# A hybrid conv/SSD trunk on one core: first z tiles from the raw x, the second block's norm from a token copy, and a hand-written order for the opening stage

## The chip, the cores and the metric

The kernel runs on one core of a Trainium2 chip. The metric is the device time in microseconds, the median of three runs. The core has TensorE (PE, matmuls; PEld is its weight load), VectorE (DVE), ScalarE (ACT), GpSimd (POOL) and SyncE (SP), which issues the DMAs. Each engine takes its instructions in the order of its own queue; semaphores tie the engines together.

## The reference

One layer and a final norm over x of 2048 tokens by 1024 channels, all in float32:

```python
def hybrid_layer(x, norm_mix_w, w_in, ...):
    h = rmsnorm(x, norm_mix_w)                 # x * rsqrt(mean(x*x) + eps) * w, per token
    proj = jnp.einsum("btd,dc->btc", h, w_in)
    u_b, u_c, u_h, z, xbc, dt_raw = jnp.split(proj, SPLITS, axis=-1)
    y_a = short_conv_mixer(u_b, u_c, u_h, short_conv_w)
    y_b = ssd_mixer(z, xbc, dt_raw, ...)       # uses silu(z) as a gate, softplus(dt_raw + dt_bias)
    x = x + jnp.einsum("btc,cd->btd", jnp.concatenate([y_a, y_b], -1), w_out)
    h = rmsnorm(x, norm_mlp_w)
    hid = jnp.square(jax.nn.relu(jnp.einsum("btd,df->btf", h, w_up)))
    return x + jnp.einsum("btf,fd->btd", hid, w_down)
```

The norm multiplies each token by one number r and each channel by a weight. So `h @ w_in` for a token is r times `(x * w) @ w_in`: the multiplication by r can be done before the projection, on its input, or after it, on its output.

## The kernel before

**Layout.** Activations lie with channels on the 128 partitions and tokens along the free axis. Tokens come in four blocks of 512, two blocks to a half. x is loaded in pieces of 128 partitions by two channel groups by 512 tokens (512 KB, 4 KB to a partition); a block has four such pieces, eight channel groups k.

**Precision.** A float32 product is made of three matmuls in a rounded format: every operand is split into a high part (a cast on ScalarE: `uh` for activations, `whi` for weights) and a low part (operand minus high part, on VectorE: `ul`, `wlo`). `mm3` (L113 to L116) issues high by high, high by low and low by high.

**Seven products.** Most of the input projection goes by pairs of column tiles in a seven-product scheme (`chain`): the two blocks of a half and the two halves of the channels form a 2x2 matrix, and four sums and differences of the operands (t1 to t4, made by `begin_sums`) stand beside the blocks b11, b21, b22. A pair has seven products named b11, t1, t2, b21, t3, b22, t4, in this order, each of 4 x 3 matmuls of 128x512 into the accumulators px, py and pw. `combine` makes the weights' sums s12 and s34 from two raw tiles on VectorE and splits them. Which pair follows which is listed in `PAIRS`; `z`, `x`, `b` and `ch` are the kinds of columns.

**The opening stage** (`Proj.start`). Four tiles of the z columns (w_in tiles 24 to 27) are computed without the seven-product scheme, as plain products of 24 matmuls for each block, so that TensorE has work before the sums exist. For each block, `begin_block` squares the four x pieces (ScalarE), adds the squares into `facc` (VectorE, eight at a time one after the other), sums over the partitions with tiny matmuls (`Rstd.reduce`, pst), takes root and reciprocal on 4 columns (`Rstd.root`), spreads the result over the partitions by two matmuls with diagonal matrices (`Rstd.spread`, prb), and copies it to SBUF. Then each channel group is scaled by weight and norm (L480), cast (L206) and split (L207). `group` runs tiles 24, 25, 26 interleaved by channel group, then tile 27, applies SiLU (L522) and stores the gates to DRAM. `dt_part` computes the 16 dt columns (pd, L604) and their softplus and cumulative sums as a chain of some 25 small operations; both blocks' chains run in the opening stage and the first pair. `begin_sums` makes the operands t1 to t4 from the scaled blocks.

**The first half** (`first_half`). The 20 pairs run with `prepare` beside them, a generator that prepares the second half: it loads x again in its channel layout, squares, adds seven times per block on VectorE (L355, L358), splits the sum (`parts`), sums and spreads it at once by two matmuls (`whole`), takes the root and a reciprocal of 128x512 (L173), then builds and stores the operands of the second half. One step of it runs after each of the seven products of a pair.

**What sets the order.** The code is recorded, and a scheduler of the framework places each engine's instructions by priority and readiness; the order in which the generators are advanced decides the priority. It may move a later operation ahead of an earlier one that would wait.

Of the kernel before, what the change touches and what calls it, by code (L numbers as in the profile page):

```python
# [11 lines left out]
F32 = mybir.dt.float32  # L12
F32R = mybir.dt.float32r
AF = mybir.ActivationFunctionType
# [25 lines left out]
def trunk(ctx: ExitStack, tc: tile.TileContext, x, w_in, w_dt, w_out, w_up, w_down, cvec, hrow, out):  # L40
# [45 lines left out]
    def col(base, i):  # L86
        return cv[:, base + i : base + i + 1]
# [21 lines left out]
    def take(it, n=None):  # L109

        return list(itertools.islice((w for w in it if w is not None), n))
# [11 lines left out]
    class Rstd:  # L123
# [17 lines left out]

        def root(self):
            n = self.n
            r = self.pool.tile([P, n], F32, tag="rs", name="rs", bufs=2)
# [47 lines left out]
    class Seven:  # L192
# [139 lines left out]
        def prepare(self, h, src, base, accs=None, held=None):  # L332
# [7 lines left out]
            for bb in range(NBB):  # L340
                if not accs:
# [64 lines left out]
    class Proj(Seven):  # L406
# [4 lines left out]
        PAIRS = "ch0 ch1 b0 x0 x8 ch2 ch3 b2 x2 ch4 ch5 b4 x4 x10 ch6 ch7 b6 x6 z4 z6".split()  # L411
# [26 lines left out]
        def bias(self):  # L438
            nc.sync.dma_start(self.hb, hrow.partition_broadcast(P))
            nc.scalar.activation(self.a_neg, self.a_neg, AF.Exp)  # L440
            nc.vector.tensor_scalar(out=self.a_neg, in0=self.a_neg, scalar1=-1.0, scalar2=None, op0=ALU.mult)
# [11 lines left out]
        def begin_block(self, bb):  # L453

            xt = self.xt[bb]
            st = Rstd(self.up, self.tmp, D, TB)
            acc = self.facc()
            for m, t in enumerate(xt):
                if bb == 0:
                    sq = self.wide("sq")  # L460
                    nc.scalar.activation(sq, t, AF.Square)
                    sq = [sq[:, 0], sq[:, 1]]
                else:
                    sq = [acc if m + i == 0 else self.tmp("sq") for i in range(2)]
                    for i in range(2):
                        nc.scalar.activation(sq[i], t[:, i], AF.Square)
                if m == 0:
                    nc.vector.tensor_tensor(out=acc, in0=sq[0], in1=sq[1], op=ALU.add)
                else:
                    for i in range(2):  # L470
                        nc.vector.tensor_tensor(out=acc, in0=acc, in1=sq[i], op=ALU.add)
                yield
            st.reduce(acc)
            st.root()
            yield
            r = st.spread(acc)
            yield
            for k in range(KD):
                t = xt[k // 2][:, k % 2]
                nc.vector.scalar_tensor_tensor(  # L480
                    out=t, in0=t, scalar=col(C_NMIX, k), in1=r, op0=ALU.mult, op1=ALU.mult
                )
                self.fill(("b11", "b21", "b12", "b22")[2 * bb + k // 4], k % 4, t)
                yield
# [28 lines left out]
        def group(self, bb, ws, tiles, work, tag="mm"):  # L513

            pm = [psum(tag, "pm", accs[tag]) for _ in tiles]
            for k in range(KD):
                for p, i in zip(pm, tiles):
                    mm3(p, ws[i][0][:, k, :], ws[i][1][:, k, :], *self.block(bb, k), k, KD)
                next(work, None)
            for p, i in zip(pm, tiles):  # L520
                o = self.tmp("z")
                nc.scalar.activation(o, p, AF.Silu)  # L522
                nc.sync.dma_start(sz_d[0][:, i, bb * TB : (bb + 1) * TB], o)

        def start(self):

            self.xt = [[self.raw("x0") for _ in range(KD // 2)], []]
            for k, t in zip(range(0, KD, 2), self.xt[0]):
                nc.sync.dma_start(t, x[0, :, k : k + 2])
            ahead = self.plain(w_in, (24, 25, 26))  # L530
            next(ahead)
            work = self.begin_block(0)
            for m in range(KD // 2):
                next(work)
            for m in range(KD // 2):
                t = self.wide("x1")
                nc.sync.dma_start(t, x[1, :, 2 * m : 2 * m + 2])
                self.xt[1].append(t)
            next(work)
            ws = []  # L540
            for _ in range(3):
                ws += take(ahead, 1)
                next(work)
            self.dt_weights()
            for _ in work:
                pass
            work = self.begin_block(1)
            last = self.plain(w_in, (27,))
            next(last)
            for bb in range(NBB):  # L550
                dts = self.dt_part(bb)
                self.group(bb, ws, (0, 1, 2), work)
                if bb == 0:
                    ws += take(last)
                    self.group(bb, ws, (3,), work, "mw")
                    self.bias()
                    for _ in dts:
                        next(work, None)
                    for _ in work:
                        pass  # L560
                    work = self.begin_sums()
                else:
                    ahead = self.weights(0, self.PAIRS[0])
                    next(ahead)
                    next(dts)
                    got = take(ahead, 3)
                    self.group(bb, ws, (3,), work, "mw")
                    got += take(ahead)
                    for _ in dts:
                        next(work, None)  # L570
                    for _ in work:
                        pass
            return got

        def dt_weights(self):
            self.dt_tiles = [self.up.tile([P, TH], F32, tag="cc", name="dts", bufs=2) for _ in range(NBB)]
            raw = self.tmp("rdt")[:, 0 : KD * 16].rearrange("p (k h) -> p k h", k=KD)
            nc.sync.dma_start(raw, w_dt)
            if self.h == 0:
# [15 lines left out]
        def dt_part(self, b):  # L595

            t = self.dt_tiles[b % NBB]
            v, e, d, p = (t[:, 64 * i : 64 * i + 64] for i in range(4))
            ct = t[:, 256:384]
            rows = t[0:64, 384:640].rearrange("p (a l) -> p a l", a=2)  # L600
# [8 lines left out]
            yield  # L609
            pt = psum("tp", "pt", 2)  # L610
# [879 lines left out]
    with ExitStack() as c1:  # L1490
# [40 lines left out]
        late = mlp.prepare(0, x1_d, C_NMLP, proj_out.accs, proj_out.raw)  # L1531
# [36 lines left out]
def _lay_out(inputs):  # L1568
# [27 lines left out]
        x=f("x")[0].reshape(NB, TB, KD, P).transpose(0, 3, 2, 1),  # L1596
        w_in=cols(w_in[:, :5632]),
# [25 lines left out]
```

## Time and profile before

| | us |
|---|---|
| median of three runs | 2651.9 |
| lowest, highest | 2649.34, 2655.21 |
| the profiled execution's own time | 2657.87 |
| its span in the trace | 2656.2 |
| busy TensorE / VectorE / ScalarE | 2602.7 / 1911.3 / 1430.8 |

Times inside the trace count from the start of the span. A timeline row gives start, duration, engine, line, operation, output and inputs, shape and a count of merged instructions; in brackets stands how long the engine idled just before and what released it. A row of the groups by shape ends with busy time, mean nanoseconds of one, and idle time before with its releaser. A row of the windows gives busy time and number of instructions of PE, PEld, DVE, ACT and POOL, then TensorE's granted clock, the share of the DMA engines, and GB/s. Matmuls overlap in the pipeline, so their spacing, not their duration, is the rate.

### The profile page before, as it was taken

The numbers are of one execution on the slowest core, as the hardware profiler recorded it, in microseconds if no ns is written. First come the engines' busy times: TensorE is split into PE (matmuls) and PEld (weight loads), VectorE is DVE, ScalarE is ACT, GpSimd is POOL, SyncE is SP. The second block draws the span as 40 slices with busy tenths as digits, with TensorE's granted clock in tenths as the row PEclk, the third lists the DMA queues.
The fourth block names the chain that finished last, engine by engine and source line by source line (L and its number), as shares of the span: only waits on it lengthen the run. The fifth ranks groups of instructions, "written<-read, shape, count | busy, mean of one in ns | idle before, by whom it ended". The sixth has DMA issues, their size and how long they took to land.

```text
span 2656.2 us, 33508 instructions
## 1 busy us (share of the span) xinstructions
PE 2602.7 (98%) x12026; PEld 2124.7 (80%) x12026; DVE 1911.3 (72%) x2586; ACT 1430.8 (54%) x2176; POOL 147.1 (6%) x162
## 2 busy tenths in 40 slices
PE   7999999999999999999999999999999999999998
PEld 5778888778877877787888888788887888888887
DVE  7997677667667666757777775755557877888985
ACT  6644345766567566767326555655555444444443
POOL 0010000011111001111000000000000000000001
PEclk9999999999999999999999999999999999999999
DMA  3585445655555578877665674654448554665762
GB/s 145 188 307 187 140 143 185 190 170 167 170 159 174 162 246 246 278 219 227 198 225 204 226 268 159 225 176 146 158 151 285 159 157 148 210 214 172 244 206 73
DMA packets 284806, 511.78 MB, mean 193 GB/s; under 512 B 25312, under 2 KB 141024, under 8 KB 284640
## 3 DMA queue, kind: packets, MB, share of 16 engines
q1 hardware_dynamic: 284640, 509.65, 57.7%
q8 instruction: 94, 1.54, 0.2%
q14 instruction: 72, 0.59, 0.1%
HBM read 344.41 MB, written 165.15 MB: 192 GB/s over the span
## 4 chain that ended last, share of the span: by engine, by line
PE 57%; issue 26%; DMA 6%; DVE 4%; ACT 4%; POOL 1%; SPq 1%; POOLq 0%; DVEq 0%; ACTq 0%
PE px L271 9%; PE px L273 9%; PE px L272 9%; PE py L271 4%; PE py L273 4%; PE py L272 4%; PE pm L114 3%; PE pm L115 3%; PE pm L116 3%; PE pw L271 2%; PE pw L272 2%; PE pw L273 2%; DMA dec<-rd_d 1%; DMA ry<-ys_d 1%; ACT whi L101 1%
## 5 line engine op out<-in xcount | busy, mean ns | idle before, releaser
L271 PE MATMUL px<-uh,whi 128*128 128x512 f32 x1672 | 658.2, 394 | 9.1 <-ACT pw L279 5.9
L273 PE MATMUL px<-uh,wlo 128*128 128x512 f32 x1672 | 652.7, 391 | 2.1 <-DVE wlo L102 2.1
L272 PE MATMUL px<-ul,whi 128*128 128x512 f32 x1672 | 652.7, 390 | 0.0
L102 DVE TENSOR_TENSOR wlo<-wraw,whi 128x1024 fp32r<-128x1024 f32 x230 | 234.0, 1017 | 228.2 <-ACT whi L101 223.0
L271 PEld LDWEIGHTS px<-uh,whi 128*128 128x128 f32 x1672 | 314.8, 188 | 84.4 <-ACT pw L279 8.0
L273 PEld LDWEIGHTS px<-uh,wlo 128*128 128x128 f32 x1672 | 314.8, 188 | 69.4 <-DVE wlo L102 2.9
L272 PEld LDWEIGHTS px<-ul,whi 128*128 128x128 f32 x1672 | 314.9, 188 | 63.9
L101 ACT CAST whi<-wraw 128x1024 fp32r<-128x1024 f32 x230 | 203.5, 885 | 282.0 <-PE px L272 194.0
L101 ACT CAST whi<-s 128x1024 fp32r<-128x1024 f32 x210 | 219.4, 1045 | 213.3 <-PE py L272 69.3
L271 PE MATMUL py<-uh,whi 128*128 128x512 f32 x836 | 327.0, 391 | 1.8 <-DVE acc L987 1.4
L272 PE MATMUL py<-ul,whi 128*128 128x512 f32 x836 | 325.6, 389 | 0.0
L273 PE MATMUL py<-uh,wlo 128*128 128x512 f32 x836 | 325.4, 389 | 0.0
L102 DVE TENSOR_TENSOR wlo<-s,whi 128x1024 fp32r<-128x1024 f32 x210 | 255.3, 1216 | 85.2 <-ACT whi L101 82.7
L114 PE MATMUL pm<-uh,whi 128*128 128x512 f32 (+1 forms) x648 | 253.2, 392 | 2.1 <-ACT uh L206 2.1
L115 PE MATMUL pm<-ul,whi 128*128 128x512 f32 (+1 forms) x648 | 249.7, 385 | 0.0
L116 PE MATMUL pm<-uh,wlo 128*128 128x512 f32 (+1 forms) x648 | 248.7, 384 | 0.0
L271 PEld LDWEIGHTS py<-uh,whi 128*128 128x128 f32 x836 | 156.9, 188 | 35.8 <-DVE acc L987 1.8
L273 PEld LDWEIGHTS py<-uh,wlo 128*128 128x128 f32 x836 | 156.8, 188 | 33.2 <-DVE wlo L102 0.4
L272 PEld LDWEIGHTS py<-ul,whi 128*128 128x128 f32 x836 | 157.0, 188 | 32.2
L271 PE MATMUL pw<-uh,whi 128*128 128x512 f32 x418 | 163.7, 392 | 0.7 <-ACT pw L279 0.7
L272 PE MATMUL pw<-ul,whi 128*128 128x512 f32 x418 | 162.9, 390 | 0.0
L273 PE MATMUL pw<-uh,wlo 128*128 128x512 f32 x418 | 162.7, 389 | 0.0
(223 smaller groups left out, 3738.6 us busy)
## 6 DMA issues: line engine op xcount, KB each, us to landing
hid_d<-e SPq DMA_DIRECT2D x96, 512.0 KB, 3.5
rh<-hid_d SPq DMA_DIRECT2D x96, 512.0 KB, 4.4
wraw<-w_in SPq DMA_DIRECT2D x68, 512.0 KB, 3.9
wraw<-w_up SPq DMA_DIRECT2D x64, 512.0 KB, 4.4
wraw<-w_down SPq DMA_DIRECT2D x104, 256.0 KB, 3.6
dec<-rd_d SPq DMA_DIRECT2D x32, 512.0 KB, 5.5
wraw<-w_out SPq DMA_DIRECT2D x32, 512.0 KB, 5.3
x_d<-xt SPq DMA_DIRECT2D x64, 256.0 KB, 3.6
```

The costliest lines, as they stand in the source:

```text
L101: nc.scalar.copy(hi, raw)
L102: eng.tensor_tensor(out=lo, in0=raw, in1=hi.bitcast(F32), op=ALU.subtract)
L114: nc.tensor.matmul(out, whi, hi, start=(k == 0), stop=False)
L115: nc.tensor.matmul(out, whi, lo, start=False, stop=False)
L116: nc.tensor.matmul(out, wlo, hi, start=False, stop=(k == nk - 1))
L271: nc.tensor.matmul(p, hi, h[0], start=bool(first and k == 0), stop=False, **kw)
L272: nc.tensor.matmul(p, hi, h[1], start=False, stop=False, **kw)
L273: nc.tensor.matmul(p, lo, h[0], start=False, stop=(k == len(g) - 1), **kw)
```

## The change

Five things, all in the opening stage but the last two.

1. The first block's four z tiles are computed from x times the weight alone (`unscaled`), without the norm. The products are multiplied by r afterwards, in PSUM or on the way to the gate (`gate`). The first block is then scaled, cast and split a second time (`scaled`) for the pairs.
2. The second block's norm is computed from a second copy of x that the host lays out with tokens on the partitions (`xt`, 128 tokens by 1024 channels). A squaring on ScalarE with a sum along the free axis (`by_token`) gives the sums without additions on VectorE and without a reduction by matmuls.
3. The opening stage's instructions are recorded under `manual_schedule`, so every engine executes them in the order in which `first_columns` writes them. The dt chains (`dt_part`) start at the end of the stage, second block first, and their remaining steps run one after each product of the first pairs.
4. In the first half, `prepare` gets the second half's norms from token copies too, with `root` and `spread` in the place of `parts` and `whole`. It starts with the second pair and advances after three of the seven products.
5. `PAIRS` begins with z4 and x0 in the place of ch0 and ch1.

```diff
     class Rstd:
...
+        def begin_tokens(self):
+            self.sums = self.pool.tile([P, self.n], F32, tag="rs", name="ssum", bufs=3)
+
+        def by_token(self, c, t):
+            nc.scalar.activation(t, t, AF.Square, accum_out=self.sums[:, c : c + 1])
...
         def prepare(self, h, src, base, accs=None, tok=None, held=None):
...
             for bb in range(NBB):
+                if tok is not None:
+                    ts = [self.raw("lt").rearrange("p a t -> p (a t)") for _ in range(TB // P)]
+                    for c, t in enumerate(ts):
+                        nc.sync.dma_start(t, tok[h * NBB + bb, c])
+                    yield
+                    yield
+                    st.begin_tokens()
+                    for c, t in enumerate(ts):
+                        st.by_token(c, t)
+                    yield
+                    st.root()
+                    yield
+                    yield
+                    rs.append(st.spread(self.facc()))
+                    yield
+                    continue
...
-        PAIRS = "ch0 ch1 b0 x0 x8 ch2 ch3 b2 x2 ch4 ch5 b4 x4 x10 ch6 ch7 b6 x6 z4 z6".split()
+        PAIRS = "z4 x0 ch0 ch1 b0 x8 ch2 ch3 b2 x2 ch4 ch5 b4 x4 x10 ch6 ch7 b6 x6 z6".split()
...
+        def unscaled(self, k):
+            i, j = WHERE["b12" if k < 4 else "b22"]
+            t = self.xt[0][k // 2][:, k % 2]
...
+            hi, lo = (a[:, j] for a in p[i])
+            nc.scalar.mul(hi, t, col(C_NMIX, k))
+            nc.vector.scalar_tensor_tensor(
+                out=lo, in0=t, scalar=col(C_NMIX, k), in1=hi.bitcast(F32), op0=ALU.mult, op1=ALU.subtract
+            )
+            return hi, lo
+
+        def scaled(self, bb, k):
+            t = self.xt[bb][k // 2][:, k % 2]
+            nc.vector.scalar_tensor_tensor(
+                out=t, in0=t, scalar=col(C_NMIX, k), in1=self.r[bb], op0=ALU.mult, op1=ALU.mult
+            )
+            self.fill(("b11", "b21", "b12", "b22")[2 * bb + k // 4], k % 4, t)
...
+        def begin_tile(self, p, w, block):
+            for k, h in enumerate(block):
+                mm3(p, w[0][:, k, :], w[1][:, k, :], *h, k, KD)
+                yield
+
+        def gate(self, bb, i, p, scale=None):
+            o = self.tmp("z")
+            if scale is not None:
+                nc.vector.tensor_tensor(out=o, in0=p, in1=scale, op=ALU.mult)
+                p = o
+            nc.scalar.activation(o, p, AF.Silu)
+            nc.sync.dma_start(sz_d[0][:, i, bb * TB : (bb + 1) * TB], o)
 
         def start(self):
...
+            with tc.manual_schedule():
+                return self.first_columns()
+
+        def first_columns(self):
...
+            load(0)
+            raws = [load_w(w_in[24])]
+            for m in range(1, KD // 2):
+                load(m)
+            raws += [load_w(w_in[24 + i]) for i in (1, 2)]
...
+            for c, t in enumerate(toks):
+                nc.sync.dma_start(t, xt[1, c])
+            raw = [self.unscaled(k) for k in range(2)]
+            ws = [split(raws[0])]
+            raw += [self.unscaled(k) for k in range(2, KD)]
+            ws.append(split(raws[1]))
+            raws.append(load_w(w_in[27]))
...
+            run(self.begin_tile(acc[0], ws[0], raw))
+            run(self.begin_tile(acc[1], ws[1], raw))
+            st = [Rstd(self.up, self.tmp, D, TB) for _ in range(NBB)]
+            st[0].reduce(sq[0][:, 0], sq[0][:, 1])
+            st[1].begin_tokens()
+            st[1].by_token(0, toks[0])
+            st[0].root()
+            ws.append(split(raws[3]))
+            st[1].by_token(1, toks[1])
+            st[1].by_token(2, toks[2])
+            tile = self.begin_tile(acc[2], ws[2], raw)
+            run(tile, 6)
+            self.r = [st[0].spread(self.facc())]
+            run(tile)
+            st[1].by_token(3, toks[3])
+            for i in range(2):
+                nc.vector.tensor_tensor(out=acc[i], in0=acc[i], in1=self.r[0], op=ALU.mult)
+            st[1].root()
+            self.scaled(0, 0)
+            tile = self.begin_tile(acc[3], ws[3], raw)
+            run(tile, 5)
+            self.r.append(st[1].spread(self.facc()))
+            run(tile)
+            for i in range(2):
+                self.gate(0, i, acc[i])
+            self.gate(0, 2, acc[2], self.r[0])
...
+            def more(k):
+                self.scaled(1, k)
+                blk.append(self.block(1, k))
+                for t in tiles:
+                    run(t, 1)
+            ahead = self.weights(0, self.PAIRS[0])
+            for k in range(4):
+                more(k)
+            self.gate(0, 3, acc[3], self.r[0])
+            next(ahead)
+            for k in range(4, KD):
+                more(k)
+                self.scaled(0, k - 3)
+            self.dt_split(rdt)
+            for k in range(5, KD):
+                self.scaled(0, k)
+            p = psum("mw", "pm", accs["mw"])
+            run(self.begin_tile(p, ws[3], blk))
+            for i in range(3):
+                self.gate(1, i, acc2[i])
+            work = self.begin_sums()
+            got = take(ahead, 1)
+            for _ in range(2):
+                next(work)
+            dts = [self.dt_part(bb) for bb in (1, 0)]
+            next(dts[0])
...
+            self.dts = itertools.chain(*dts)
             return got
...
         def first_half(self, ws):
             self.last_sums()
-            late = self.prepare(1, x, C_NMIX)
+            late = self.prepare(1, x, C_NMIX, tok=xt)
...
                 def after(name):
-                    next(late, None)
+                    next(self.dts, None)
+                    if m and name in ("b11", "t2", "t3"):
+                        next(late, None)
...
+        xt=f("x")[0].reshape(NB, TB // P, P, D),
```

More of the change, by code (lines that the diff above doesn't have):

```diff
@@ L39, in trunk @@
 @with_exitstack
-def trunk(ctx: ExitStack, tc: tile.TileContext, x, w_in, w_dt, w_out, w_up, w_down, cvec, hrow, out):
+def trunk(ctx: ExitStack, tc: tile.TileContext, x, xt, w_in, w_dt, w_out, w_up, w_down, cvec, hrow, out):
     nc = tc.nc
@@ L450, in wide @@
             return self.e(name).rearrange("p (a t) -> p a t", a=2)
[L453 to L484, printed above, removed]
+        def unscaled(self, k):
+            i, j = WHERE["b12" if k < 4 else "b22"]
+            t = self.xt[0][k // 2][:, k % 2]
+            p = self.places[k % 4]
+            p[i] = self.place(i)
+            hi, lo = (a[:, j] for a in p[i])
[10 more added lines that the diff above has]
+            self.fill(("b11", "b21", "b12", "b22")[2 * bb + k // 4], k % 4, t)
         def begin_sums(self):
@@ L511, in begin_sums @@
                     yield
[L513 to L523, printed above, removed]
@@ L609, in dt_part @@
             yield
+            t = self.up.tile([P, TH], F32, tag="cc", name="dts", bufs=2)
+            v, e, d, p = (t[:, 64 * i : 64 * i + 64] for i in range(4))
+            ct = t[:, 256:384]
+            rows = t[0:64, 384:640].rearrange("p (a l) -> p a l", a=2)
             pt = psum("tp", "pt", 2)
```

96 lines of the change are left out of this document (44 added, 52 removed).

## The prediction

> **What bounds the kernel now.** I read the page's head, then the timeline of the first 100 us on three engines, the groups by shape for durations, and the windows for where TensorE is short of work.
>
> ```profile
> PE 2602.7 (98%) x12026; PEld 2124.7 (80%) x12026; DVE 1911.3 (72%) x2586; ACT 1430.8 (54%) x2176; POOL 147.1 (6%) x162
> ```
> ```profile
> 19.41 1.65 PE L114 MATMUL pm<-uh,whi 128*128 128x512 f32 x3 [2.11 <-ACT uh L206]
> ...
> 22.13 0.63 PE L116 MATMUL pm<-uh,wlo 128*128 128x512 f32 x1
> 22.56 0.63 PE L115 MATMUL pm<-ul,whi 128*128 128x512 f32 x1
> ...
> 29.67 0.39 PE L114 MATMUL pm<-uh,whi 128*128 128x512 f32 x1
> ...
> 31.71 0.39 PE L114 MATMUL pm<-uh,whi 128*128 128x512 f32 x1
> ...
> 38.51 0.95 PE L133 MATMUL pst<-ones_r,facc 128*128 128x1 f32 x8
> ...
> 45.35 0.40 PE L604 MATMUL pd<-uh,wdt 128*32 128x512 f32 x1
> ...
> 49.07 0.40 PE L114 MATMUL pm<-uh,whi 128*128 128x512 f32 x1
> ...
> 76.17 0.50 PE L271 MATMUL px<-uh,whi 128*128 128x512 f32 x1
> ```
>
> TensorE is the bound: whatever idles it is lost. Its first product starts at 19.41. Matmuls start 0.43 us apart at first (22.13 to 22.56) and later 0.227 apart (nine from 29.67 to 31.71). From 19.41 to 45.35 it computes the first block's four z tiles (96 matmuls), the sums of the second block's norm (x8 at 38.51) and one spreading of a norm; the pairs begin at 76.17. A pair is seven products of 12 matmuls, 84 x 0.227 = 19.1, so the first pair ends near 95.6.
>
> ```profile
> 140.00:160.00 20.00, 19.34 (x85) 15.71 (x85) 13.83 (x21) 7.71 (x10) 1.88 (x3) 1.00 0.87 330
> 160.00:180.00 20.00, 18.13 (x78) 14.30 (x77) 20.00 (x25) 9.40 (x11) 2.95 (x4) 1.00 0.88 319
> 180.00:200.00 20.00, 19.42 (x86) 15.74 (x85) 19.85 (x26) 9.21 (x13) 2.85 (x3) 1.00 0.89 330
> 200.00:220.00 20.00, 19.74 (x87) 16.02 (x86) 16.95 (x22) 9.92 (x13) 2.65 (x4) 1.00 0.74 263
> ```
>
> In these windows (busy PE, PEld, DVE, ACT, POOL) VectorE is full from 160 to 200, and TensorE lacks 0.66 + 1.87 + 0.58 + 0.26 = 3.4 us. That is the second stretch the change can touch.
>
> **A: the earlier start, -11.5.** What a first product needs now is x, one weight tile and its splits, no norm.
>
> ```profile
> 5.55 1.06 ACT L461 ACTIVATE sq<-x 128x1024 f32<-128x1024 f32 x1 [3.27 <-DMA x<-x]
> ...
> 9.44 1.06 ACT L461 ACTIVATE sq<-x 128x1024 f32<-128x1024 f32 x1 [0.18 <-DMA x<-x]
> 10.69 1.04 ACT L101 CAST whi<-wraw 128x1024 fp32r<-128x1024 f32 x1 [0.20 <-DMA wraw<-w_in]
> ```
> ```profile
> L207 DVE TENSOR_TENSOR ul<-x,uh 128x512 fp32r<-128x512 f32 x32 | 21.0, 683 | 0.5 <-ACT uh L206 0.4
> L480 DVE SCALAR_TENSOR_TENSOR x<-x,cv,facc 128x512 f32<-128x512 f32 x16 | 11.1, 745 | 2.9 <-ACT facc L182 2.9
> L102 DVE TENSOR_TENSOR wlo<-wraw,whi 128x1024 fp32r<-128x1024 f32 x12 | 14.6, 1218 | 2.8 <-ACT whi L101 2.8
> L206 ACT CAST uh<-x 128x512 fp32r<-128x512 f32 x32 | 18.1, 618 | 4.7 <-DVE x L480 3.1 <-DVE x L210 1.5
> L522 ACT ACTIVATE z<-pm 128x512 f32<-128x512 f32 x8 | 4.5, 600 | 0.0
> ```
>
> Pieces of 512 KB land 1.3 us apart: the four x pieces from 5.5 to 9.4, a weight at 10.7. The weight is now second in the queue, so it lands near 6.8. ScalarE makes two scaled copies (about 0.65 each) by 6.9 and the weight's cast (1.04) by 7.9: the first matmul starts there, 11.5 before 19.41. VectorE's eight low parts and two weight splits (8 x 0.745 + 2 x 1.22 = 8.4 from 6.2) end near 14.6, ahead of a cold tile of 24 x 0.43 = 10.3. The cold stretch is paid in both kernels.
>
> The squares of x leave the path. Four token copies (2 MB) now go ahead of the fourth weight and the second x block: 5.2 us at 1.3 per piece, so the weight lands near 20 and the block by 25, before their uses at 23 and 34. A squaring with its sum is not in this trace; I bound it by 1.06 and 1.06 plus the shortest ScalarE row, about 0.2, take the upper, and both are hidden. The square root of the first norm waits for TensorE's sums at 23, with a weight's cast and three squares queued behind it on ScalarE; tile 3, which needs that weight, comes at 29, so this wait is free. SyncE's weight loads for the first pair stand behind the fourth gate's store, near 47, and are needed near 68: free.
>
> From 7.9 the four tiles take the 25.9 of 19.41 to 45.35, plus eight more sums (0.8) and a second spreading (0.5), plus 0.3: they end near 35.4, 10.0 earlier.
>
> **B: the second block's first operand, +2.5.** Its norm is spread ahead of the last nine matmuls, at 35.4 - 2.0 = 33.4.
>
> ```profile
> 39.78 1.28 ACT L522 ACT_TABLE_LOAD   x1
> 41.07 0.60 ACT L522 ACTIVATE z<-pm 128x512 f32<-128x512 f32 x1
> ```
>
> Behind the copy of the norm (0.6, to about 34.4) ScalarE has in its written order: this table load (1.28), three gates (0.6 each, 0.52 apart), and then the first high part (0.62): 37.9. TensorE waits 2.5. The Trainium skill, ScalarE: Activation LUTs, section "What ACT_TABLE_LOAD costs", charges a change of tables about 2.66 us, a drain of 1.38 included. By it B would be 3.9. The rows show none: the function starts at 41.07, 1.29 after the load.
>
> **C: the written order on VectorE, +7.1.** The scheduler before grouped VectorE's work:
>
> ```profile
> 17.95 0.75 DVE L480 SCALAR_TENSOR_TENSOR x<-x,cv,facc 128x512 f32<-128x512 f32 x1 [0.37 <-ACT facc L182]
> ...
> 44.13 2.08 DVE L480 SCALAR_TENSOR_TENSOR x<-x,cv,facc 128x512 f32<-128x512 f32 x3 [2.56 <-ACT facc L182]
> 46.13 1.89 DVE L207 TENSOR_TENSOR ul<-x,uh 128x512 fp32r<-128x512 f32 x3
> ```
> ```profile
> 18.74 0.62 ACT L206 CAST uh<-x 128x512 fp32r<-128x512 f32 x1 [0.29 <-DVE x L480]
> ```
>
> Three scalings, then three low parts: ScalarE's casts ran beside them. In the new order every scaling is followed by its own low part, which waits for ScalarE's cast of that piece, and the next scaling is queued behind that wait. One link is 0.745 + 0.04 (18.70 to 18.74) + 0.62 + 0.04 + 0.60 (three low parts in 1.89) = 2.04, of which VectorE idles 0.7. TensorE's nine matmuls on a piece also take 2.04, so pieces 0 to 3 just keep pace. At piece 4 a gate's multiplication (0.6) comes in between, and from there a first-block link stands before each second-block link: 4.08 per piece against 2.04. Pieces 5 to 7 lose 2.04 each, piece 4 0.6, and the last low part 0.4: 7.1. The last piece's high part is ready at 37.9 + 3 x 2.04 + 2.64 + 3 x 4.08 = 58.9 and the 72 matmuls end near 61.4. The fourth tile (24 x 0.227 = 5.5) and two dt projections (3.7 each, 45.35 to 49.07) follow: the pairs begin near 74.3, against 76.17 (the 1.6 of sums and spreading added ahead are made up by small dt matmuls that move into the pairs). Of A's 11.5 only 1.9 is left.
>
> **D: the first pair starves, +12.9.**
>
> ```profile
> 83.54 0.68 DVE L207 TENSOR_TENSOR ul<-x,uh 128x512 fp32r<-128x512 f32 x1
> ```
> ```profile
> L631 DVE SCALAR_TENSOR_TENSOR dts<-dts 128x64 f32<-128x64 f32 x14 | 3.1, 219 | 0.0
> ```
>
> Before, VectorE made the low part of the pair's last operand (t4) by 84.2, and TensorE came to it near 92.8: 8 us of cover. After, VectorE leaves the second block at 59.5, does four more first-block links (8.2) and the dt weights (0.5): 68.2. The next weight's cast stands behind three gates on ScalarE, its split ends at 71.4. Up to t4's last low part VectorE's list then has 38 operations of 128x512 (0.60 to 0.69: subtractions, additions, low parts, weight sums; 0.62 x 38 = 23.6), two weight splits and a half one (2.9), some 19 small dt operations (about 0.2 each, 4.0), and waits of about 2: 32.5, so 103.9. The t4 product (12 x 0.227 = 2.7) ends the pair at 106.6: 32.3 from 74.3, where a pair takes 19.4 now, and 11.0 after 95.6. A to D come to -11.5 + 2.5 + 7.1 + 12.9 = +11.0.
>
> **E: the second pair, +3.8.** The dt chains now run inside the first pairs. From 104 ScalarE has three squares (1.26 each), four table loads (1.28), gates, casts and small functions: about 13, to 117, before it frees an accumulator that TensorE wants near 113.2 (106.6 + 24 matmuls + the small ones). Bounds: 0, if its list is done sooner, to 6.
>
> **F: the later stage's norms, -3.4.**
>
> ```profile
> L358 DVE TENSOR_TENSOR facc<-facc,lx 128x512 f32<-128x512 f32 x12 | 8.2, 682 | 0.0
> L173 DVE RECIPROCAL facc<-facc 128x512 f32<-128x512 f32 x2 | 6.7, 3347 | 0.0
> L153 DVE TENSOR_TENSOR diag<-ident,rs 128x512 fp32r<-128x512 f32 x4 | 2.6, 685 | 0.0
> ```
>
> The additions (8.2) and wide reciprocals (6.7) go; four diagonals (2.6) and small operations (1) come: VectorE saves about 11, and the steps are spread over three of seven products instead of all. I take back all 3.4 of the windows above; bounds 0 and 3.4.
>
> **G: the clock, +1.**
>
> ```profile
> 2034.14 0.50 PE L271 MATMUL py<-uh,whi 128*128 128x512 f32 x1 [1.39 <-DVE acc L987]
> ...
> 2035.30 0.62 PE L271 MATMUL px<-uh,whi 128*128 128x512 f32 x1 [0.19 <-DVE acc L987]
> 2035.72 0.63 PE L272 MATMUL px<-ul,whi 128*128 128x512 f32 x1
> ...
> 2038.70 0.51 PE L273 MATMUL px<-uh,wlo 128*128 128x512 f32 x1
> ```
> ```profile
> 2035.00:2040.00 5.00, 4.81 (x15) 3.71 (x15) 0.30 (x2) 0.00 (x0) 0.00 (x0) 0.66 1.02 379
> ```
>
> After idle times of 1.39 and 0.19 matmuls fall to 0.43 apart for 3.4 us, at a granted clock of 0.66 in that window. C makes TensorE half idle for 12 us. While pieces come 4.08 apart, nine slow matmuls (3.9) still fit; a slow stretch costs only where it outlasts the starved one, up to 1.7 (3.4 x a half) each time. I take 1; bounds 0 and 4. The Trainium skill, TensorE: Matmul & The Clock Gate, Part 1, section "What's actually happening", halves the clock only after a whole idle window of about 3.4 us. By it G is 0 and the sum 11.4. The rows decide: the drop came after shorter gaps.
>
> **Sum.** 11.0 + 3.8 - 3.4 + 1 = +12.4 on the profiled execution's 2657.9 (span 2656.2): 2670.3. That execution is 6.0 above the median of the runs, so the median goes from 2651.9 to 2664.3.
>
> **The rivals.** *Faster: VectorE passes its waits.* If VectorE worked on while ScalarE casts, a link would cost its own 0.66 + 0.60 = 1.26. Then 16 links give back 12.5 and D's waits 2: the last low part comes at 89.4, the pair ends at 92.1 instead of 95.6 (-3.5), E and G are 0, F stays: 2645.0. It decides when a link is under about 1.35. For it: the early start is real, and ScalarE is little more than half busy. Against: the written order, and the 2.56 us that VectorE stands before 44.13 until ScalarE's copy comes. Chance 0.08. *No change:* D's list is 8 us shorter than I count, because operations of it fit into gaps, and E is 0: 11.0 - 8 - 3.4 + 1 = +0.6, 2652.5. Chance 0.06. *Worse: the clock stays down.* Gaps recur in the second block and in the first pair, G is 4, and ScalarE's list in E, at its upper bound, costs 6: 2669.5. It decides if slow stretches reach into the fourth tile and the first pair. Chance 0.16. *The forecast:* 0.70.
>
> **The numbers.** Downward: E 0 (-3.8), G 0 (-1), and 3.5 of D's waits and small operations hidden: 2656. Upward: E 6 (+2.2), G 4 (+3), F 0 (+3.4), and 0.08 instead of 0.04 per hand-over, twice in 16 links (+1.3): 2674. This range leaves out the two rivals below it, 0.14, and holds the others. About 0.2%, 5.3 us, is what a measurement can tell from none. Only the first rival is faster by that much (0.08); the second and the lower edge of the forecast are the same (0.07); slower 0.85.
>
> **What would show it.** Right: first matmul near 8; TensorE waiting about 2.5 for the second block's first piece; VectorE idle some 0.7 before each low part, pieces 4.1 us apart; the first pair from 74 to 107; VectorE not full from 160 to 200. Wrong: pieces under 3 us apart, or a first pair that takes 20 us.

## The result and the profile after

| | before | after |
|---|---|---|
| median, us | 2652.24 (2649.34 to 2655.21, 6 runs) | 2671.69 (2667.58 to 2675.33, 6 runs) |
| the profiled execution, us | 2657.87 | 2670.82 |
| its span, us | 2656.2 | 2668.8 |

The ratio is 1.0066, with a 95% interval from 1.0055 to 1.0076: the change costs 17.5 us of 2652, and 14.6 to 20.2 by the interval. The two medians of the table alone are 19.45 apart, which lies inside that interval. The two profiled executions are 12.95 apart, since the one of before was 5.6 above its median and the one of after 0.9 below. A part below goes into what lies between.

The page of after, engines, and the timeline of TensorE over the opening stage and the first pair:

```profile
PE 2609.4 (98%) x12026; PEld 2128.8 (80%) x12026; DVE 1905.8 (71%) x2579; ACT 1437.7 (54%) x2194; POOL 140.1 (5%) x162
```
```profile
8.32 0.80 PE L114 MATMUL pm<-uh,whi 128*128 128x512 f32 x1 [8.32 <-ACT whi L101]
...
37.26 0.50 PE L114 MATMUL pm<-uh,whi 128*128 128x512 f32 x1 [2.06 <-ACT uh L213]
...
50.16 0.50 PE L114 MATMUL pm<-uh,whi 128*128 128x512 f32 x1 [1.30 <-ACT uh L213]
...
54.28 0.50 PE L114 MATMUL pm<-uh,whi 128*128 128x512 f32 x1 [1.28 <-ACT uh L213]
...
58.42 0.50 PE L114 MATMUL pm<-uh,whi 128*128 128x512 f32 x1 [1.30 <-ACT uh L213]
...
60.27 0.63 PE L116 MATMUL pm<-uh,wlo 128*128 128x512 f32 x1
60.70 0.63 PE L114 MATMUL pm<-uh,whi 128*128 128x512 f32 x1
...
75.53 0.39 PE L278 MATMUL px<-uh,whi 128*128 128x512 f32 x1
...
81.65 0.49 PE L279 MATMUL py<-ul,whi 128*128 128x512 f32 x1 [2.20 <-DVE ul L214]
...
104.05 0.58 PE L278 MATMUL px<-uh,whi 128*128 128x512 f32 x1
...
108.27 0.47 PE L278 MATMUL px<-uh,whi 128*128 128x512 f32 x1
...
117.44 0.50 PE L278 MATMUL px<-uh,whi 128*128 128x512 f32 x1 [3.44 <-ACT pw L286]
```

The first product starts 11.1 earlier than before's 19.41, the second block's first piece is waited for (37.26), and its last three pieces come 4.1 apart (50.16, 54.28, 58.42). After these gaps matmuls run 0.43 apart for a while (60.27 to 60.70). The pairs begin at 75.53, only 0.6 earlier than before, and soon wait again for a low part (81.65). The cause stands in VectorE's timeline of the same kernel:

```profile
52.79 0.74 DVE L491 SCALAR_TENSOR_TENSOR x<-x,cv,facc 128x512 f32<-128x512 f32 x1
54.26 0.69 DVE L214 TENSOR_TENSOR ul<-x,uh 128x512 fp32r<-128x512 f32 x1 [0.73 <-ACT uh L213]
54.87 0.75 DVE L491 SCALAR_TENSOR_TENSOR x<-x,cv,facc 128x512 f32<-128x512 f32 x1
56.31 0.69 DVE L214 TENSOR_TENSOR ul<-x,uh 128x512 fp32r<-128x512 f32 x1 [0.69 <-ACT uh L213]
...
101.69 2.50 DVE L214 TENSOR_TENSOR ul<-x,uh 128x512 fp32r<-128x512 f32 x4
...
107.44 0.68 DVE L797 TENSOR_TENSOR eb<-px,s 128x512 f32<-128x512 f32 x1
```

Scaling, idle, low part, scaling, idle, low part: from 52.79 to 54.87 one link is 2.08, of which VectorE stands 0.73 and waits for a cast that ScalarE could only start when the scaling was done. The row at 101.69 is t4's four low parts; they end at 104.2. The last row reads px as t3 left it; t4 adds to px too and can only start behind that (108.27). ScalarE's timeline of after, from there to the copy that frees the second pair's accumulator:

```profile
104.40 1.06 ACT L147 ACTIVATE lt<-lt 128x1024 f32<-128x1024 f32 x1 [1.71 <-DMA lt<-xt]
105.36 0.19 ACT L147 ACTIVATION_READ_ACCUMULATOR lt<-lt 128x1 f32 x1
105.57 1.28 ACT L732 ACT_TABLE_LOAD   x1
...
109.52 1.28 ACT L814 ACT_TABLE_LOAD   x1
...
111.47 1.28 ACT L711 ACT_TABLE_LOAD   x1
...
113.03 1.28 ACT L820 ACT_TABLE_LOAD   x1
...
116.80 0.59 ACT L286 COPY pw<-px 128x512 f32<-128x512 f32 x1
```

From 104.40 on, four table loads and three squares stand ahead of the copy at 116.80, among gates and casts, and TensorE's 3.44 before 117.44 is the wait for it. The windows of after (busy PE, PEld, DVE, ACT, POOL, then the granted clock):

```profile
80.00:100.00 20.00, 15.55 (x54) 10.94 (x55) 19.48 (x42) 13.83 (x23) 1.95 (x2) 0.85 0.33 119
100.00:120.00 20.00, 16.18 (x58) 12.12 (x58) 16.38 (x39) 18.16 (x29) 0.00 (x0) 0.84 0.71 247
...
160.00:180.00 20.00, 20.00 (x90) 16.53 (x89) 11.93 (x14) 7.05 (x9) 1.69 (x3) 1.00 0.34 115
180.00:200.00 20.00, 20.00 (x89) 16.52 (x88) 14.87 (x21) 6.02 (x9) 0.00 (x0) 1.00 0.52 200
```

From 80 to 100 VectorE is full and TensorE has 54 matmuls where 88 would fit; from 100 to 120 ScalarE is nearly full. From 160 to 200, where VectorE was full before, it has 26.8 of 40, and TensorE lacks nothing.

**A ruler for the whole span.** ScalarE copies one accumulator to `pw` once in every pair (`combine`'s caller, L279 before, L286 after), 109 times in the span. The start of the n-th copy, less that of before, tells how far a kernel is behind or ahead at that pair. A copy also moves a little when the scheduler runs a product out of turn, so a difference counts that stays from column to column. In before the copies of pairs 1, 2, 20 and 21 start as follows, read from ScalarE's timeline:

```profile
81.29 0.58 ACT L279 COPY pw<-px 128x512 f32<-128x512 f32 x1
...
102.14 0.58 ACT L279 COPY pw<-px 128x512 f32<-128x512 f32 x1
...
448.96 0.57 ACT L279 COPY pw<-px 128x512 f32<-128x512 f32 x1 [1.88 <-PE px L273]
...
470.02 0.59 ACT L279 COPY pw<-px 128x512 f32<-128x512 f32 x1
```

Differences to before in us (minus: ahead):

| kernel | pair 1 | 2 | 3 | 5 | 8 | 20 | 21 | 24 | ratio, 95% interval |
|---|---|---|---|---|---|---|---|---|---|
| after | +1.6 | +14.7 | +16.2 | +16.9 | +12.4 | +12.4 | +16.4 | +17.8 | 1.0066 [1.0055, 1.0076] |
| e1_skew | -9.1 | +3.8 | +3.8 | +4.8 | +0.3 | +0.3 | +3.9 | +5.0 | 1.0018 [1.0009, 1.0028] |
| e2_auto | -4.3 | -4.9 | -0.2 | +0.3 | -3.4 | -3.5 | +0.5 | +1.7 | 1.0002 [0.9993, 1.0010] |
| e3_tok_only | +0.2 | +0.5 | -0.3 | +0.9 | -4.3 | -4.3 | -3.9 | -4.0 | 0.9981 [0.9972, 0.9991] |
| e4_oldlate | +2.7 | +15.7 | +17.8 | +18.7 | +14.2 | +15.2 | +19.3 | +20.5 | 1.0069 [1.0056, 1.0082] |
| e5_old_pairs | +1.7 | +8.7 | +15.4 | +15.3 | +11.0 | +11.0 | +11.2 | +12.0 | 1.0045 [1.0028, 1.0061] |
| e6_dts_later | +1.5 | +11.2 | +14.0 | +14.1 | +9.7 | +9.6 | +13.1 | +14.4 | 1.0068 [1.0054, 1.0082] |
| e7_fill | +1.9 | +15.4 | +15.3 | +16.2 | +11.7 | +11.7 | +16.1 | +16.2 | 1.0071 [1.0057, 1.0085] |
| x8_skew_then_scheduler | -8.1 | -7.8 | -6.3 | -6.1 | -10.6 | -10.7 | -6.6 | -6.6 | 0.9982 [0.9971, 0.9994] |
| x9_skew_scheduler_pairs | -7.3 | -9.3 | -7.8 | -5.8 | -10.2 | -9.0 | -8.9 | -9.2 | 0.9962 [0.9948, 0.9976] |
| x10_skew_pairs | -9.4 | -5.1 | +1.0 | +2.8 | -1.6 | -1.6 | -0.1 | +0.1 | 0.9991 [0.9982, 1.0000] |

The columns come from one execution each, the ratio from repeated runs of a kernel beside runs of before on the same chip. Kernels are compared by their ratios, since the median of before was between 2652.2 and 2657.5 in the four rounds of measurement. One of the six executions of e5_old_pairs ran at a mean granted clock of 0.849 and took 2896.8; its figures here are those of the other five. From pair 24 on the code is the same in all kernels, and yet the differences of single executions move by up to 7 us there: x10's is +0.1 at pair 24 and +2.4 at the last pair, after's +17.8 and +12.0, x8's -6.6 and -13.8. So the two profiles can differ by 12.95 where the runs differ by about 17.5.

### The profile page after: what moved, and what is told of

It is laid out like the page before. It is cut to its first block, busy times and chain, and to the rows that moved or that the text cites. A ratio compares the mean times of both kernels' runs of the same rounds, so it can differ in the third digit from the quotient of the medians.

```text
span 2668.8 us, 33533 instructions
## 1 busy us (share of the span) xinstructions
PE 2609.4 (98%) x12026; PEld 2128.8 (80%) x12026; DVE 1905.8 (71%) x2579; ACT 1437.7 (54%) x2194; POOL 140.1 (5%) x162
## 4 chain that ended last, share of the span: by engine, by line
PE 60%; issue 26%; DMA 5%; ACT 4%; DVE 4%; POOL 1%; SPq 0%; POOLq 0%; ACTq 0%; DVEq 0%
PE px L278 9%; PE px L280 9%; PE px L279 9%; PE py L278 4%; PE py L279 4%; PE py L280 4%; PE pm L114 3%; PE pm L116 3%; PE pm L115 3%; PE pw L278 2%; PE pw L280 2%; PE pw L279 2%; DMA dec<-rd_d 1%; ACT whi L101 1%; PE yd L1357 1%
## 5 line engine op out<-in xcount | busy, mean ns | idle before, releaser
L278 PE MATMUL px<-uh,whi 128*128 128x512 f32 x1672 | 660.8, 395 | 17.1 <-ACT pw L286 12.9
L279 PE MATMUL px<-ul,whi 128*128 128x512 f32 x1672 | 655.0, 392 | 0.8 <-DVE ul L214 0.8
L278 PEld LDWEIGHTS px<-uh,whi 128*128 128x128 f32 x1672 | 316.0, 189 | 93.9 <-ACT pw L286 15.4
L279 PEld LDWEIGHTS px<-ul,whi 128*128 128x128 f32 x1672 | 316.3, 189 | 66.1 <-DVE ul L214 1.8
L279 PE MATMUL py<-ul,whi 128*128 128x512 f32 x836 | 325.7, 390 | 2.2 <-DVE ul L214 2.2
L279 PEld LDWEIGHTS py<-ul,whi 128*128 128x128 f32 x836 | 157.0, 188 | 34.7 <-DVE ul L214 2.5
L279 PE MATMUL pw<-ul,whi 128*128 128x512 f32 x418 | 163.0, 390 | 0.0
```

What stands on the lines that cost most here:

```text
L278: nc.tensor.matmul(p, hi, h[0], start=bool(first and k == 0), stop=False, **kw)
L279: nc.tensor.matmul(p, hi, h[1], start=False, stop=False, **kw)
```

## The experiments

**e1_skew: the one-piece shift.** The written order stays, but every scaling is written ahead of the low part of the piece before it.

```diff
-        def scaled(self, bb, k):
+        def scaled(self, bb, k, then=None):
...
+            if then is not None:
+                self.scale(*then)
...
             for k in range(4, KD):
-                more(k)
-                self.scaled(0, k - 3)
+                more(k, (0, k - 3))
+                self.scaled(0, k - 3, (1, k + 1) if k + 1 < KD else (0, 5))
```

> Edit: in the second block's loop each scaling on VectorE is written ahead of the low part of the piece before it; nothing else moves. Theory (the written order starves VectorE): a link falls from 2.04 to about 1.27 us, the pieces from number 4 on come 2.5 apart instead of 4.1, the pairs begin near 68 instead of 75.5, and 16 links give 12 us back to VectorE's list, so the first pair ends near 97 instead of 108: about 10 us less than the changed kernel, 2661. Rival 1 (the work itself: the first block is scaled and split a second time, and VectorE has too much to do in any order): the pairs begin earlier, but the first pair still ends near 106: 2 us less or nothing, 2670. Rival 2 (the dt chains and table loads on ScalarE in the first pairs are the cost): under 3 us less.

Median 2662.03, ratio 1.0018. VectorE's timeline:

```profile
47.55 0.68 DVE L214 TENSOR_TENSOR ul<-x,uh 128x512 fp32r<-128x512 f32 x1
48.15 0.74 DVE L490 SCALAR_TENSOR_TENSOR x<-x,cv,facc 128x512 f32<-128x512 f32 x1
48.81 0.68 DVE L214 TENSOR_TENSOR ul<-x,uh 128x512 fp32r<-128x512 f32 x1
49.42 0.74 DVE L490 SCALAR_TENSOR_TENSOR x<-x,cv,facc 128x512 f32<-128x512 f32 x1
```

The same instructions with no idle time: a link takes 1.27 (48.15 to 49.42) instead of 2.04 to 2.08. The pairs begin at 67.20, 8.3 earlier than in after, and at pair 20 the kernel is 12.1 ahead of after; by the ratios it gets back 4.8 of the 6.6 thousandths. So the idle time in the written order is the largest single part of the loss, and the work that the change adds is not. What is left is the stretch from the first pair's copy to the second's, which still takes 12.9 longer (from -9.1 at pair 1 to +3.8 at pair 2).

**e2_auto: no written order.**

```diff
-            with tc.manual_schedule():
-                return self.first_columns()
+            return self.first_columns()
```

> Edit: the same code without the written order, so that the scheduler places the opening stage's instructions. Theory (the written order): VectorE's scalings and low parts are grouped as in the kernel before, the links lose their waits, and the first pair ends near 92 to 95: 14 to 17 us less than the changed kernel, 2655 to 2658. Rival 1 (the work itself is too much): the first pair ends after 103, under 4 us less. Rival (the raw x is worth nothing without the written order): the first z matmul comes near 19 as before and the time is that of before or more.

Median 2656.49, ratio 1.0002. The early start is there (first product at 8.31), and the first pair doesn't starve: -4.3 at pair 1, -4.9 at pair 2. But the scheduler puts the second block's norm and its first operand late, as TensorE's timeline shows:

```profile
37.38 0.50 PE L186 MATMUL prb<-diag,ones_r 128*128 128x512 f32 x1 [2.15 <-DVE diag L160]
...
41.88 1.22 PE L114 MATMUL pm<-uh,whi 128*128 128x512 f32 x2 [3.99 <-ACT uh L213]
```

Its pairs begin at 73.74, 2.4 earlier than in before; of the 11.1 of the early start, 6.1 go in these two waits. The early start thus doesn't need the written order, and the scheduler's largest waits lie elsewhere than those of the written order. At the passage from pair 20 to 21 it loses another 4.0, as after does; where the rest goes was not tried.

**e3_tok_only and e4_oldlate: the later norms alone, and the rest alone.** e3 is before with the token copies in `prepare` at its old pace (an advance after every product). e4 is after with the old norms, at the new pace:

```diff
-            late = self.prepare(1, x, C_NMIX, tok=xt)
+            late = self.prepare(1, x, C_NMIX)
```

> Edit: the kernel before with one part of the change alone, the second half's norms from token copies in the first half, at the old pace. Theory (part F of the prediction): VectorE is relieved by about 11 us between 100 and 220 and TensorE's waits there go: 3 to 4.5 us less than before, 2648 to 2649. Rival (F is not the token copies but the slower pace and later start): 0 to 1 us less.

> Edit: the changed kernel with the second half's norms from x in channel layout, with seven additions per block on VectorE, at the new pace. Theory (part F is the token copies): VectorE is full again somewhere between 130 and 230, TensorE waits there, 3 to 4 us more than the changed kernel, 2675. Rival (F is the pace: three steps in seven products, begun with the second pair): no change within 1.5 us.

e3: median 2652.07, ratio 0.9981, faster by 5. e4: 2676.2, ratio 1.0069. Windows of e3, then of e4:

```profile
160.00:180.00 20.00, 20.00 (x89) 16.19 (x88) 19.95 (x24) 11.87 (x14) 2.80 (x4) 1.00 0.80 298
180.00:200.00 20.00, 20.00 (x90) 16.57 (x89) 18.43 (x23) 9.43 (x12) 1.71 (x2) 1.00 0.88 316
```
```profile
160.00:180.00 20.00, 20.00 (x90) 16.36 (x89) 16.88 (x19) 9.84 (x13) 0.83 (x3) 1.00 0.35 113
180.00:200.00 20.00, 20.00 (x90) 16.58 (x89) 11.00 (x15) 5.73 (x8) 0.00 (x0) 1.00 0.50 186
```

In both TensorE lacks nothing from 160 to 200. Token copies at the old pace take the 3.4 us away, and so does the new pace with the old norms; e4 is 2.8 behind after at pair 20, 1.1 of it from pair 1 on, and the ratios don't tell the two apart. So the 3.4 go by either part of the change, and the second part adds at most 3 more.

**e5_old_pairs: the list of before.**

```diff
-        PAIRS = "z4 x0 ch0 ch1 b0 x8 ch2 ch3 b2 x2 ch4 ch5 b4 x4 x10 ch6 ch7 b6 x6 z6".split()
+        PAIRS = "ch0 ch1 b0 x0 x8 ch2 ch3 b2 x2 ch4 ch5 b4 x4 x10 ch6 ch7 b6 x6 z4 z6".split()
```

> Edit: the changed kernel with the old list of pairs (ch0 ch1 b0 x0 first, z4 z6 last). Theory (part E of the prediction, ScalarE's table loads between gates, exponentials and roots in the first two pairs): without gates there the wait of 3.4 us and the slow stretch behind it (118.4 to 121.3) go, 4 us less than the changed kernel, 2667. A second effect: at the end of the first half two z pairs stand before the second half again instead of x6 and z6, and the passage to the second half (from the 20th copy of an accumulator to the 21st: 25.1 us after, 21.1 before) is 4 us shorter. Rival (E is the dt chains whatever the pair): no change in the first pairs.

Median 2668.3, ratio 1.0045. Up to pair 20 it gains 1.4; the second pair is earlier, but by the third the two kernels are 0.8 apart, so the list doesn't settle what the first pairs lose. The gain lies where the half ends. ScalarE's timeline there, of after and then of e5:

```profile
461.32 0.57 ACT L286 COPY pw<-px 128x512 f32<-128x512 f32 x1 [0.51 <-PE px L280]
...
485.50 1.04 ACT L328 CAST uh<-rb 128x1024 fp32r<-128x1024 f32 x1 [1.24 <-DMA rb<-hm_d]
486.45 0.58 ACT L286 COPY pw<-px 128x512 f32<-128x512 f32 x1
```
```profile
459.91 0.57 ACT L286 COPY pw<-px 128x512 f32<-128x512 f32 x1 [1.88 <-PE px L280]
...
481.20 0.59 ACT L286 COPY pw<-px 128x512 f32<-128x512 f32 x1
```

From copy to copy after takes 25.1, e5 21.3 and before 21.1. In the last pair of the list the operands of the later half are read back and split (`rb`), on the same two engines. In after the pair ahead of it is x6, whose convolution then falls into the same stretch. VectorE's and TensorE's timelines of after:

```profile
459.85 4.87 DVE L752 SCALAR_TENSOR_TENSOR cacc<-buf,cv,cacc 128x1024 f32<-128x1024 f32 x4
464.63 1.22 DVE L329 TENSOR_TENSOR ul<-rb,uh 128x1024 fp32r<-128x1024 f32 x1
```
```profile
487.08 0.80 PE L278 MATMUL px<-uh,whi 128*128 128x512 f32 x1 [3.89 <-ACT pw L286]
487.68 0.63 PE L279 MATMUL px<-ul,whi 128*128 128x512 f32 x1
488.10 0.63 PE L280 MATMUL px<-uh,wlo 128*128 128x512 f32 x1
```

VectorE's first split of `rb` stands behind four steps of that convolution, 3.3 after the copy, and at the end the copy that frees TensorE's accumulator stands behind a cast that waits for its DMA: TensorE idles 3.89, and a slow stretch follows. In the old list z4 stands there, which has no convolution. That the list costs most of these 4 us is shown, here and in x9 and x10 below; that it is the convolution is read from the rows and wasn't tried by itself.

**e6_dts_later: the dt steps start with the second pair.**

```diff
                 def after(name):
-                    next(self.dts, None)
+                    if m:
+                        next(self.dts, None)
```

> Edit: the changed kernel with the remaining steps of the dt chains begun with the second pair instead of the first. Theory (dt operations in VectorE's list for the first pair count, part D, and ScalarE's list, part E): the first pair ends near 105 instead of 108 (4 us of small operations leave its list), the second pair takes as long or longer, since the chains and the table loads are then in it: 0 to 3 us less. Rival (the dt chains are the main cost of the first two pairs): 6 us less or more.

Median 2674.8, ratio 1.0068. At pair 2 it is 3.5 ahead of after and at pair 20 2.8, but the runs show no gain: the small operations are a minor part of what the first pair loses, and less than these runs can tell.

**e7_fill: the clock.** Matmuls whose result isn't used fill the places where TensorE is half idle: six a piece while pieces come 4.1 apart, and three a step in product t2 of the first pair.

```diff
+                        if self.warm and name == "t2":
+                            self.spin(3, h[0])
...
+        def spin(self, n, h):
+            pw = ps.tile([P, 512], F32, tag="yo", name="spin", bufs=1)
+            for _ in range(n):
+                nc.tensor.matmul(pw, ones_r, h, start=True, stop=True)
...
+                if 4 <= k < KD - 1:
+                    self.spin(6, blk[k][0])
```

> Edit: the changed kernel with matmuls that nobody reads, where TensorE was half idle: six after each of the pieces 4 to 6 of the second block (1.4 of the 2.0 us that it waits), three after each channel group of the first pair's t2. Theory (the clock: half idle stretches throttle TensorE): the slow stretches at 60.3 to 63 and at 94.4 to 104 are gone, the pairs begin 1.4 earlier at 74.1, t3 and b22 take 2.7 each, and the first pair ends 2 to 3 us earlier, bounded by VectorE's last low part at 104: 2 to 3 us less. Rival (VectorE alone sets the end of the first pair): matmuls fast, end unchanged within 1 us. Rival (the throttle needs a whole idle window): the slow stretches stay as they are.

Median 2676.2, ratio 1.0071. The window from 92 to 104, of after and then of e7:

```profile
92.00:104.00 12.00, 10.06 (x25) 6.91 (x25) 12.00 (x22) 8.29 (x14) 0.59 (x1) 0.59 0.43 144
```
```profile
92.00:104.00 12.00, 8.75 (x36) 6.15 (x36) 12.00 (x22) 8.50 (x15) 0.58 (x1) 1.00 0.43 137
```

The granted clock is 1.00 instead of 0.59, and the slow stretch in the second block is gone too (from 60 to 63.5 it is 1.00 instead of 0.51): the pairs begin at 74.28 instead of 75.53.

```profile
74.28 0.39 PE L278 MATMUL px<-uh,whi 128*128 128x512 f32 x1
```

But VectorE is full in both windows, with the same 22 instructions, and at pair 5 the kernel is only 0.7 ahead of after. So VectorE sets the first pair's end, and taking these two slow stretches away gains under 1 us in this execution and nothing in the ratio. The clock isn't up throughout: from 104 to 112 it is lower in e7 than in after. The window in after, then in e7:

```profile
104.00:112.00 8.00, 7.63 (x34) 5.67 (x33) 5.67 (x14) 7.53 (x13) 0.00 (x0) 0.97 0.71 250
```
```profile
104.00:112.00 8.00, 6.69 (x19) 5.18 (x20) 6.20 (x15) 6.82 (x12) 0.00 (x0) 0.58 0.75 248
```

What a clock that is up all the time would bring stays open.

**x8_skew_then_scheduler, x9_skew_scheduler_pairs, x10_skew_pairs: what the findings add up to.** x8 is e1 with the written order ended behind the second block's tiles and gates; operand sums, dt chains and the first weights' splits are left to the scheduler. x9 is x8, and x10 is e1, with the list of before.

```diff
             with tc.manual_schedule():
-                return self.first_columns()
+                got = self.first_columns()
+            return self.rest_columns(*got)
```

> Edit: the skewed order of the second block (each scaling ahead of the low part of the piece before), and the written order ends with the last scaling; the sums, the weights of the first pair and the dt chains are left to the scheduler. Theory (two written orders starve TensorE, the one in the second block and the one around the sums and dt chains): the pairs begin near 68, VectorE's list for the first pair is interleaved by readiness, the first pair ends near 88 to 90 and the time is 18 to 20 us below the changed kernel and 3 to 6 us below before. Rival (the sums' order is harmless, what is left is VectorE's and ScalarE's work): no better than the skew alone, which stood 12 to 13 us below the changed kernel.

> Kernel x8 with the list PAIRS of the kernel before, nothing else. If the 4 us between pair 20 and 21 belong to the new list (its last two entries x6 z6 instead of z4 z6), they go here too: the first 20 pairs keep what x8 had (about -10.7 against the kernel before at pair 20), the 21st stands at the same difference within 0.5, and the median comes 4 below x8's, near 2646, ratio about 0.9966. Rival: the 4 us are paid somewhere in any case (the norm or the steps of the later half have to be done by then): the difference at pair 21 is again 4 smaller, ratio 0.998. Second rival: the new list also helps the first pair (a z pair first needs no sums for the convolution), so that the difference at pair 2 is worse here than x8's -7.8 by 2 or more; then the two cancel.

> Kernel e1 (the written order kept to its end, each scaling ahead of the low part of the piece before) with the list PAIRS of the kernel before. e1 stood at +0.3 against the kernel before at pair 20 and +3.9 at pair 21, ratio 1.0018. If the list costs the passage: +0 to +0.5 at pair 21, ratio about 1.0004. If the passage is paid in any case: +4 at pair 21, ratio 1.0018. If the old list costs the first pairs of a written order something: more than +0.3 at pair 20.

x8: median 2650.27, ratio 0.9982. Its pairs begin at 69.18 and the first pair no longer starves: -8.1 at pair 1, -7.8 at pair 2, where e1 goes from -9.1 to +3.8. It still pays 4.1 at the passage from pair 20 to 21. x9: median 2648.16, ratio 0.9962; it keeps its -9.0 through the passage, so the rival (paid in any case) falls, and so does the second rival, since pair 2 stands at -9.3. x10: 2654.3, ratio 0.9991, against e1's 1.0018, with 1.5 instead of 3.6 at the passage, so there the list isn't the whole of it. With the list of before the ratio falls each time: by 2.1 thousandths from after to e5, 2.7 from e1 to x10, 2.0 from x8 to x9; only for e1 and x10 do the intervals stand apart, the other two overlap. x9 is the fastest kernel here, 0.38% under before.

## Why the prediction was right, and which terms were off

The forecast was 2664.3 with a range from 2656 to 2674; the median is 2671.7. The direction, the mechanism of the opening stage and the sizes of nearly all the terms stand; one cost was missing.

- **A, -11.5:** the first product came at 8.32, not 7.9: -11.1.
- **B, +2.5:** 2.06, at 37.26 for 37.9.
- **C, +7.1, and G, +1:** links of 2.04 to 2.08, pieces 4.1 apart, as worked out. A slow stretch follows; without it (e7) the pairs begin at 74.28, the 74.3 of the forecast; with it at 75.53. G was right in size, but e7 gave most of that 1.2 back in the first pair, whose end VectorE sets.
- **D, +12.9, and E, +3.8:** t4's last low part ends at 104.2 (forecast 103.9). TensorE then waits 3.44 for ScalarE's list at 117.44. From the beginning of the pairs (0.6 ahead) to pair 3 (16.2 behind) the loss is 16.8, against 16.7 of the two terms. (The prediction counts a pair as 19.1 in one place and 19.4 in another; by the first D would be 13.2.) The path differs from the forecast's: the pair was to end with t4 at 106.6, but TensorE ran the second pair's first product from 104.05 on and t4 only from 108.27, behind VectorE's addition at 107.44, to 111.1. It came to the place where it waits for ScalarE at 113.8, forecast 113.2. e1 and x8 show whose the loss is: the shift alone leaves it, ending the written order takes it away. So D and E together aren't the amount of work in the first pair but the order in which it stands, which the prediction had not separated. x8 changes that order on all engines at once; which engine's order counts most wasn't tried.
- **F, -3.4:** -4.5 between pairs 5 and 8. The prediction put it down to fewer operations and slower pace together; either is enough (e3, e4).
- **The sum, +12.4,** is just what after is behind at pair 20. That it agrees to the tenth is partly luck: the pairs began 0.3 later than A, B, C and G give, 0.7 more went between pairs 3 and 5, and F was 1.1 larger.
- **What was missing: +4.0 at the passage of the halves.** The prediction treated the new list only by what it does to the first pair, and gave no term to its end, where x6 now stands next to last. e5 and x9 take the loss away, x10 more than half of it. With it the sum is +16.4, within the interval of the runs.
- **From which execution to count.** The sum was made against an execution 6.0 above the median, and the differences were taken over to the median unchanged. That holds: 2651.9 + 16.4 is 2668.3, 3.4 under the median of after. What remains is within the up to 7 us by which single executions move behind pair 24.

The rivals: VectorE didn't pass its waits (0.69 to 0.74 idle before each low part), and the list in the first pair wasn't shorter. Of the third, the slow clock did reach into the first pair (0.59 from 92 to 104), but e7 took that stretch away and gained next to nothing; its time, 2669.5, was closer to the result than the forecast's, for a reason that isn't its own.

## What to carry to other kernels

When an order is written by hand for in-order engines, write an operation that waits for another engine behind the independent work of the next piece: here a shift by one piece was worth 12 us at pair 20 (e1), and a written order that ended earlier 11 more (x8). An earlier start of one stage gains only what the engine that feeds the next stage can follow. When a list of stages is reordered, look at its end as well as its beginning: here the last two entries decided what fell into the passage to the next stage.

## What the hardware showed that was not expected

TensorE's granted clock fell though no gap in the 12 us before was longer than 1.30: three gaps of 1.28 to 1.30, each with one of 0.22 to 0.23 behind it, were followed by matmuls 0.43 apart (60.27 and 60.70), at a granted clock of 0.51 from 60 to 63.5. The single gap of 2.06 at 37.26 wasn't: from 36 to 48 the clock was 1.00. The Trainium skill, TensorE: Matmul & The Clock Gate, Part 1, section "What's actually happening", wants a whole idle window of about 3.4 us for that; this trace disagrees, as before's did. Matmuls without use held the clock at 1.00 in the same places (e7). A squaring with its sum took 1.06 and a second instruction of 0.19 (104.40, 105.36), the upper of the two bounds that the prediction had for it.
